# Rows of V at 144 bytes instead of 132, and a planner with other constants, in a multi-query attention kernel

## The chip, the core and the metric

The kernel runs on one core of a Trainium2 chip. The metric is the device time of one execution in microseconds (us). The core has five engines that run beside each other and meet at semaphores: TensorE (PE, matrix products), VectorE (DVE), ScalarE (ACT), GpSimd (POOL) and SyncE (SP, which here only issues transfers). Matrix products are written to PSUM, everything else that is kept on the chip lies in SBUF, both with 128 partitions.

## The reference

Multi-query attention: 8 batches, 1024 positions, 16 query heads of 64 columns, and one K and one V per batch that all heads share. All inputs and the output are float32.

```python
batch, seq_len, embed_dim = (8, 1024, 1024)
num_heads = 16
head_dim = embed_dim // num_heads
...
scores = np.matmul(q, k.transpose(0, 1, 3, 2)) / np.sqrt(head_dim)
weights = np.exp(scores - np.max(scores, axis=-1, keepdims=True))
weights = weights / np.sum(weights, axis=-1, keepdims=True)
attn_out = np.matmul(weights, v)
```

## The kernel before

**Units.** Heads are worked in pairs. A unit is one pair, one chunk of 512 queries and one key tile of 128 keys; there are 8 batches x 8 pairs x 2 chunks x 8 key tiles = 1024 of them. `scores` (L256) makes the scores of a unit with two matmuls (one per head, 64 rows of the array each, L263) into a PSUM tile of 128 keys x 1024 queries; there are three such tiles. No maximum is subtracted; sums out of range are detected at the end and sent to a general path that this input does not take.

**Two ways to the exponential.** A unit goes to ScalarE or to VectorE. ScalarE takes one instruction (`scalar_exp`, L276) and leaves one fp16 weight tile, "wt". VectorE builds the exponential from the bits of the scaled score: `ve_bits` (L283) reads the PSUM tile and writes the integer form, `ve_mantissa` (L294) and `ve_power` (L304) cut it apart, `ve_square` (L315) squares the mantissa, and the product of mantissa square and value, the cube, is made in two parts, the first columns by GpSimd (`ve_cube`, L319) and the rest by VectorE (`ve_rest`, L327). What comes out are three weight tiles in one buffer, "we", which enter the value product with the factors 1, C0 and C3.

**Values.** V of a batch lies in SBUF as `vps`, a tile of [128 keys, 3 terms, 8 key tiles, row], where the three terms are V, C0 x V and C3 x V (`prep_v`, L251), and each row holds 64 columns of V and a column of the term's factor, which makes the sum of the weights beside the product. `value` (L387, matmul at L396) multiplies 128 x 128 weights by 65 columns of such a row. An output group (128 queries of one head) is the sum of 8 products for the eight key tiles, in the order of the key tiles, and of two more for each key tile that VectorE made: first the terms C0 of all these, then the terms C3. Seven groups share a PSUM bank, and there are two such banks. `inverse` (L345) takes the reciprocal of the sums of a bank and `finish` (L354) multiplies the seven groups by it, both on VectorE; SP stores the result.

**The order.** All instructions are issued in an order that `plan` (L467) works out when the kernel is built, with a model of durations in its constants: T_MM for a value product, T_ACT, VE_COST and so on. TensorE's stream alternates between scores of one to three units and a burst of value products. The constants that set the order, as far as the change touches them:

- N_W3 buffers for VectorE's weight tiles, RATE the greatest share of units that VectorE gets, VE_SLACK the backlog up to which VectorE is given a further one.
- NEXT: how long VectorE may stand idle for a pass that is not ready yet rather than take another one. HOLD: `ve_bits` is not preferred over the unfinished passes of an earlier unit until the time to that unit's square is above HOLD.
- MINC the fewest columns of a cube that GpSimd is given, REST the remainder at or under which VectorE takes the rest itself.
- WAIT: when a score tile may be issued if one only is free, against the time at which ScalarE runs dry. SAFE: how long after its modelled readiness a weight tile may be used by a value product.

`load_v` is issued by POOL at unit 30 of the batch before, `prep_v` comes due at unit 72 (SIDE).

Of the kernel before, what the change touches and what calls it, by code (L numbers as in the profile page):

```python
# [11 lines left out]
FP16 = mybir.dt.float16  # L12
# [10 lines left out]
C3 = 0.163818359375  # L23
CS = 2.1471603163479376
N_WT = 22
N_W3 = 7
N_M = 2
N_M2 = 3
T_PAIR = 214.0
T_IN = 96.0  # L30
T_OUT = 106.0
T_MM = 30.8
T_SCORE = 480.0
T_ACT = 917.0
ACT_DONE = 1110.0
# [19 lines left out]
    "finish": 542.0,  # L55
}
ORDER = {"bits": 0, "inverse": 1, "finish": 2}
NEXT = {"bits": 0.0, "inverse": 0.0, "finish": 120.0}
MINC = 96
REST = 640  # L60
LATE = 500.0
VSLOT = 1
DEFER = 12
HOLD = 700.0
VE_SLACK = 2100.0
V_END = 12
RATE = 0.225
NEAR = 2000.0
WAIT = 50.0
T_BITS = 1255.0  # L70
SAFE = 0.0


@with_exitstack
def attention_main(ctx, tc, q, k, v, out, flag):
# [13 lines left out]
    P = 128  # L89
    NKT = S // P  # L90
# [13 lines left out]
    consts = ctx.enter_context(tc.tile_pool(name="consts", bufs=1))  # L104
# [12 lines left out]
    ident16 = consts.tile([P, P], FP16, name="ident16")  # L117
    ones = consts.tile([P, 1], FP32, name="ones")
    rec_all = consts.tile([P, NG], FP32, name="rec_all")
    vps = [consts.tile([P, 3, NKT, 66], FP16, name=f"vp{i}") for i in range(2)]  # L120
    ok_all = consts.tile([P, B + GRP], FP32, name="ok_all")
    qf = consts.tile([P, NKT, P], FP32, name="qf")

# [343 lines left out]
    def plan():  # L467
        ops = []

        def emit(t, what, *args):  # L470
            ops.append((t, len(ops), what, args))
# [10 lines left out]
        wt_used = [0.0] * N_WT  # L482
        w3_used = [0.0] * N_W3
        m_used = [0.0] * N_M
# [26 lines left out]
        def late_free(i):  # L511

            if free[i] < float("inf"):
                return free[i]
            return max(t_ve, min(x[1] for x in todo)) + T_BITS

        def backlog():

            t = sum(VE_COST[k] for k, _ in chain) + VE_COST["rest"] * len(left)
            return t + sum(VE_COST[k] for _, k, _, _ in evict)  # L520

        def share(s):
# [5 lines left out]
            if v is not None:  # L528
                gs = max(t_gp, t_behind + GP_START, squared[v] + GP_START)
                n = min(int((s - gs - GP_FIX) / GP_COL) // 32 * 32, left[v])  # L530
                if n >= MINC:
                    lo = 2 * QCH - left[v]
# [12 lines left out]
        def vector_step(limit):  # L545
# [4 lines left out]
            for x in [(r, "bits", v, 0) for v, r in todo] + evict:  # L550
                r, what = x[:2]
                s = max(t_ve, r, min(w3_used) if what == "bits" else 0.0)
                key = (max(s, t_ve + NEXT[what]), ORDER[what], x[2])
                if best is None or key < best[0]:
                    best = (key, s, x)
            urgent = best is not None and (
                best[1] <= t_ve + NEXT[best[2][1]]
                and (best[2][1] == "bits" or behind is not None or best[2][0] < t_ve - LATE or not chain)
            )
            if urgent and best[2][1] == "bits" and not any(left.values()):  # L560
                t = 0.0
                for what, v in chain:
                    t += VE_COST[what]
                    if what == "square":
                        urgent = t > HOLD
                        break
            if not urgent and (
                chain or left and (flush or left[next(iter(left))] <= REST or u - next(iter(left)) > DEFER)
            ):
                what, v = chain[0] if chain else ("rest", next(iter(left)))  # L570
                old = next(iter(left), None)
                if old is not None and (
                    left[old] <= REST
                    or what == "square"
# [74 lines left out]
        def issue(t, first):  # L649
# [6 lines left out]
                and not todo  # L656
                and max(t_ve, s) + backlog() < s + T_SCORE + VE_SLACK
                and kinds.get(u - 1) != "V"
                and made_v < (u - NKT + 1) * RATE
                and min(w3_used) < s  # L660
# [35 lines left out]
        while h < H or u < STEPS:  # L696
# [7 lines left out]
            if n_free == 1:  # L704
                other = sorted(late_free(i) for i in range(3))[1]
                go = max(other, t_pe) + T_IN + T_SCORE > t_act + WAIT and t_pe + NEAR >= t_act - T_IN - T_SCORE
            if u < STEPS and go:
# [15 lines left out]
            if terms is not None:  # L723
# [3 lines left out]
                if r < float("inf"):  # L727
                    r += SAFE
                if n == 0 and gg % GB == 0:
                    r = max(r, bank_free[gg // GB % 2])  # L730
                if r <= t_pe:
                    s = t_pe + (T_OUT if mode == "s" else 0)
                    mode = "v"
                    emit(s, "value", gg, n)
                    t_pe = s + T_MM
                    n += 1
# [185 lines left out]
@with_exitstack  # L922
def kernel(ctx, tc, q, k, v, out):
    nc = tc.nc
    fp = ctx.enter_context(tc.tile_pool(name="flagp", bufs=1))
    flag = fp.tile([1, 1], I32, name="flag")
    attention_main(tc, q, k, v, out, flag)
    bad = nc.values_load(flag, min_val=0, max_val=1)
    with tc.If(bad != 0):
        attention_general(tc, q, k, v, out)  # L930
# [30 lines left out]
```

## Time and profile before

| what | us |
|---|---|
| median of 3 runs | 769.5 (769.27 to 770.57) |
| the profiled execution | 769.24 |
| its span, first to last instruction | 767.5 |
| PE busy | 753.1 |
| ACT busy | 748.6 |
| DVE busy | 733.0 |
| POOL busy | 360.0 |

In a row of a group, the names are output<-inputs, then the shapes, the count after the x, and behind the bar the busy time in us, the mean duration in ns and the idle time ahead of it with what ended that. A row of a timeline or of the chain of waits begins with its start and its length in us. PE's durations overlap, since matmuls are pipelined: the distance of two starts says what one costs, not its duration. The same holds for the passes of VectorE and ScalarE, whose ends overlap with the next start by some 80 to 120 ns. The granted TensorE clock was 0.998 of full speed.

### The profile page before, as it was taken

The numbers are of one execution on the slowest core, as the hardware profiler recorded it, in microseconds if no ns is written. First come the engines' busy times: TensorE is split into PE (matmuls) and PEld (weight loads), VectorE is DVE, ScalarE is ACT, GpSimd is POOL, SyncE is SP. The second block draws the span as 40 slices with busy tenths as digits, with TensorE's granted clock in tenths as the row PEclk, the third lists the DMA queues.
The fourth block names the chain that finished last, engine by engine and source line by source line (L and its number), as shares of the span: only waits on it lengthen the run. The fifth ranks groups of instructions, "written<-read, shape, count | busy, mean of one in ns | idle before, by whom it ended". The sixth has DMA issues, their size and how long they took to land.

```text
span 767.5 us, 31677 instructions
## 1 busy us (share of the span) xinstructions
PE 753.1 (98%) x13842; PEld 486.4 (63%) x13842; DVE 733.0 (96%) x1467; ACT 748.6 (98%) x804; POOL 360.0 (47%) x314
## 2 busy tenths in 40 slices
PE   6999999999999999999999999999999999999996
PEld 3556666666666666666666666666666666666665
DVE  3999999999999999999999999999999999999994
ACT  7999999999999999999999999999999999999994
POOL 4554444545445535444555443545444444444440
PEclk9999999999999999999999999999999999999999
DMA  9976427654356634795447552487544676212122
GB/s 182 153 110 109 91 66 119 111 112 98 78 98 111 114 71 95 95 133 92 83 86 119 113 112 70 92 112 114 105 77 93 101 120 100 58 44 57 30 57 73
DMA packets 168926, 73.91 MB, mean 96 GB/s; under 512 B 94032, under 2 KB 161616, under 8 KB 168784
## 3 DMA queue, kind: packets, MB, share of 16 engines
q1 hardware_dynamic: 149152, 53.76, 35.5%
q0 software_dynamic: 18576, 17.57, 17.9%
q8 instruction: 109, 1.79, 1.0%
q10 hardware_dynamic: 1056, 0.52, 0.3%
q14 instruction: 33, 0.27, 0.1%
HBM read 37.75 MB, written 33.55 MB: 93 GB/s over the span
## 4 chain that ended last, share of the span: by engine, by line
PE 95%; ACT 2%; DVE 1%; DMA 1%; issue 0%
PE ot L396 57%; PE sc L263 38%; ACT wt L276 2%; DMA qf<-in_q_dram 1%; DVE we L283 0%; PE otl L420 0%; DVE osb L354 0%; PE qps L216 0%; DVE rec_all L345 0%; ACT q_first L799 0%; DVE mm L315 0%; ACT qt L229 0%; DVE we L304 0%; DVE m L294 0%; PE cnt L837 0%
## 5 line engine op out<-in xcount | busy, mean ns | idle before, releaser
L276 ACT ACTIVATE wt<-sc 128x1024 f16<-128x1024 f32 x801 | 746.1, 1040 | 4.5 <-PE sc L263 3.6
L319 POOL TENSOR_TENSOR we<-we,mm 128x864 f16<-128x864 f16 (+5 forms) x229 | 315.4, 1377 | 386.3 <-DVE mm L315 148.2
L396 PE MATMUL ot<-vp,wt 128*128 128x65 f16 x6344 | 441.3, 194 | 0.0
L396 PE MATMUL ot<-vp,we 128*128 128x65 f16 x5352 | 431.3, 194 | 0.0
L396 PEld LDWEIGHTS <-wt 128*128 128x128 f16 x6344 | 323.4, 98 | 129.2 <-issue 129.2
L396 PEld LDWEIGHTS <-we 128*128 128x128 f16 x5352 | 313.0, 97 | 92.0 <-issue 89.7
L263 PE MATMUL sc<-qt,k2t 64*128 64x512 f16 x2048 | 353.0, 386 | 3.5 <-ACT wt L276 2.8
L283 DVE TENSOR_SCALAR we<-sc 128x1024 int16<-128x1024 f32 x223 | 272.0, 1220 | 6.0 <-PE sc L263 4.3
L315 DVE TENSOR_TENSOR mm<-m 128x1024 f16<-128x1024 f16 x223 | 152.4, 683 | 0.1
L263 PEld LDWEIGHTS <-k2t 64*128 64x128 f16 x2048 | 77.8, 93 | 46.8 <-issue 7.0
L354 DVE TENSOR_TENSOR osb<-ot,rec_all 128x448 f32<-128x448 f32 x146 | 90.8, 622 | 4.9
L294 DVE TENSOR_SCALAR m<-we 128x1024 int16<-128x1024 int16 x223 | 95.1, 427 | 0.3
L304 DVE TENSOR_SCALAR we<-we 128x1024 int16<-128x1024 int16 x223 | 93.4, 419 | 0.0
L327 DVE TENSOR_TENSOR we<-we,mm 128x160 f16<-128x160 f16 (+5 forms) x219 | 78.2, 357 | 0.1
L166 POOL DMA_DIRECT2D q<-in_q_dram x64 | 38.6, 604 | 2.1 <-DMA q_first<-in_q_dram 1.7
L345 DVE RECIPROCAL rec_all<-ot 128x7 f32<-128x7 f32 x146 | 29.0, 198 | 6.4 <-PE ot L396 5.5
L149 POOL DMA_DIRECT2D vp<-in_v_dram x8 | 7.2, 900 | 0.0
L200 PE MATMUL kps<-ident,k 128*64 128x128 f16 x16 | 1.3, 314 | 4.5 <-DVE k L191 4.5
L251 DVE TENSOR_SCALAR vp<-vp 128x512 f16<-128x512 f16 x16 | 3.9, 286 | 1.5 <-DMA vp<-in_v_dram 1.5
L229 DVE COPY qt<-qps 128x512 f16<-128x512 f16 (+1 forms) x2 | 1.1, 555 | 4.0 <-PE qps L216 4.0
L234 DVE TENSOR_SCALAR k16d<-knat 128x1024 f16<-128x1024 f32 x7 | 4.8, 684 | 0.0
L200 PEld LDWEIGHTS <-k 128*64 128x64 f16 x16 | 0.8, 158 | 4.7 <-DVE k L191 4.7
(30 smaller groups left out, 23.5 us busy)
## 6 DMA issues: line engine op xcount, KB each, us to landing
out_dram<-osb SPq DMA_DIRECT2D x109, 256.0 KB, 2.7
q<-in_q_dram POOLq DMA_DIRECT2D x56, 256.0 KB, 4.6
out_dram<-osb SPq DMA_DIRECT2D x38, 128.0 KB, 2.6
knat<-in_k_dram SPq DMA_DIRECT2D x7, 256.0 KB, 3.3
q<-in_q_dram POOLq DMA_DIRECT2D x8, 192.0 KB, 7.5
vp<-in_v_dram POOLq DMA_DIRECT2D x8, 128.0 KB, 6.6
qt<-q SPq DMA_TRANSPOSE x64, 5.2
qf<-in_q_dram ACTq DMA_DIRECT2D x2, 256.0 KB, 4.4
```

The lines of the kernel that those rows point to most:

```text
L166: nc.gpsimd.dma_start(out=q16[(b, c)], in_=q[b, c * P : (c + 1) * P, h0:, :].rearrange("p h d -> p (h d)"),)
L263: nc.tensor.matmul(sc[u][:, hh, :], k2t[r : r + 64, j * P : (j + 1) * P], qt[b][r : r + 64, p % HP, c * QCH : (c + 1) * QCH], start=True, ...
L276: nc.scalar.activation(out=w, in_=sc.pop(u), func=EXP, scale=escale, bias=math.log(CS))
L283: nc.vector.tensor_scalar(out=w3[:, 1].bitcast(I16), in0=sc.pop(u), scalar1=15.0 * 1024, scalar2=0.0, op0=ALU.add, op1=ALU.max,)
L294: return nc.vector.tensor_scalar(out=ve[u]["m"].bitcast(I16), in0=ve[u]["w3"][:, 1].bitcast(I16), scalar1=0x3FF, scalar2=0x3C00, op0=ALU.b ...
L304: return nc.vector.tensor_scalar(out=ve[u]["w3"][:, 0].bitcast(I16), in0=ve[u]["w3"][:, 1].bitcast(I16), scalar1=0x7C00, scalar2=None, op0 ...
L315: return nc.vector.tensor_tensor(out=ve[u]["m2"], in0=m, in1=m, op=ALU.mult)
L319: x = nc.gpsimd.tensor_tensor(out=wu[:, lo:hi], in0=we[:, lo:hi], in1=mm[:, lo:hi], op=ALU.mult)
L327: return nc.vector.tensor_tensor(out=wu[:, lo:], in0=we[:, lo:], in1=mm[:, lo:], op=ALU.mult)
L345: nc.vector.reciprocal(out=rec_all[:, g0 : g0 + n], in_=o[:, 0:n, D])
L354: nc.vector.tensor_tensor(out=ob[:, i0 : i0 + n, :], in0=o[:, 0:n, 0:D], in1=rec.unsqueeze(2).broadcast_to([P, n, D]), op=ALU.mult,)
L396: nc.tensor.matmul(ots[g0][:, gg - g0, 0 : D + 1], w[:, hh, qb * P : (qb + 1) * P], kv[h // (HP * NCH)]["vp"][:, ci, u % NKT, 0 : D + 1], ...
```

## The change

The rows of `vps` become 72 columns of fp16 long, 144 bytes, where they were 66 columns, 132 bytes; the columns that are written and read stay the same 65. The tile starts at a multiple of 64 bytes in both kernels. The constants of the planner change with it, and so does the order of nearly all instructions behind the first units.

```diff
-N_W3 = 7
+N_W3 = 8
...
-T_MM = 30.8
+T_MM = 29.6
...
-NEXT = {"bits": 0.0, "inverse": 0.0, "finish": 120.0}
-MINC = 96
-REST = 640
+NEXT = {"bits": 0.0, "inverse": 0.0, "finish": 0.0}
+MINC = 128
+REST = 768
...
-HOLD = 700.0
-VE_SLACK = 2100.0
+HOLD = 1400.0
+VE_SLACK = 2500.0
...
-RATE = 0.225
+RATE = 0.235
...
-WAIT = 50.0
+WAIT = -100.0
...
-SAFE = 0.0
+SAFE = 300.0
...
-    vps = [consts.tile([P, 3, NKT, 66], FP16, name=f"vp{i}") for i in range(2)]
+    vps = [consts.tile([P, 3, NKT, 72], FP16, name=f"vp{i}") for i in range(2)]
```

What the order of the built programs holds, counted:

| | before | after |
|---|---|---|
| units of ScalarE / VectorE | 801 / 223 | 800 / 224 |
| value products (L396) | 11,696 | 11,712 |
| bursts of them | 733 | 744 |
| score runs of 1 / 2 / 3 units | 453 / 276 / 2 | 475 / 264 / 4 |
| GpSimd cubes (L319): instructions, columns | 229, 144,320 | 279, 121,888 |
| VectorE rests (L327): instructions, columns | 219, 84,032 | 222, 107,488 |
| `finish` directly behind `inverse` | 145 | 7 |
| bits pass directly behind a square | 117 | 147 |

## The prediction

> **What bounds the kernel now.** I read the page first (shares, chain, groups), then the windows of the steady part, the chain of waits piece by piece, and last the timeline of single engines.
>
> ```profile
> span 767.5 us, 31677 instructions
> PE 753.1 (98%) x13842; PEld 486.4 (63%) x13842; DVE 733.0 (96%) x1467; ACT 748.6 (98%) x804; POOL 360.0 (47%) x314
> PE 95%; ACT 2%; DVE 1%; DMA 1%; issue 0%
> L276 ACT ACTIVATE wt<-sc 128x1024 f16<-128x1024 f32 x801 | 746.1, 1040 | 4.5 <-PE sc L263 3.6
> L396 PE MATMUL ot<-vp,wt 128*128 128x65 f16 x6344 | 441.3, 194 | 0.0
> L396 PE MATMUL ot<-vp,we 128*128 128x65 f16 x5352 | 431.3, 194 | 0.0
> L263 PE MATMUL sc<-qt,k2t 64*128 64x512 f16 x2048 | 353.0, 386 | 3.5 <-ACT wt L276 2.8
> ```
> ```profile
> 100.00:700.00 600.00, 600.00 (x11133) 388.68 (x11128) 591.21 (x1181) 597.09 (x641) 287.80 (x240) 1.00 0.55 96
> ```
>
> (The window's columns are length, then busy time of PE, weight loads, DVE, ACT, POOL, then clock and DMA.) Three engines are 98% busy or more, but the chain that ended last is PE for 95%, and PE's scores waited 3.5 us in all. So TensorE sets the end; ACT and DVE are just behind it. A matmul's 194 ns is its pipelined length, not what it costs; the cost is the distance between starts, which the chain of waits shows, since its pieces run from start to start:
>
> ```profile
> 470.65 0.54 PE sc L263 x4
> 471.19 1.32 PE ot L396 x39
> 472.52 0.54 PE sc L263 x4
> 473.05 0.39 PE ot L396 x9
> 473.45 0.32 PE sc L263 x2
> 473.77 0.63 PE ot L396 x17
> ```
>
> From x9 (0.385, the mean of the 0.38 and 0.39 that such pieces show) to x39 (1.32) is 0.935 us for 30 value products: **31.2 ns each**, and 1.32 - 39 x 0.0312 = 0.10 us for each burst, whatever its length. A unit's two score matmuls alone cost 0.32 us, two units together 0.54.
>
> **What the padding does.** A row of vp is the moving operand of one value product. In both kernels vp starts at a multiple of 64 bytes. With 132-byte rows, key tile j starts at phase 0, 4, 8, 12, 0, 4, 8, 12 of a 16-byte grid for j = 0 to 7 (each of the three term blocks repeats this); with 144 bytes every row starts at phase 0. The trace before already holds sequences of equal phase, because a group of products ends with the extra terms of the DVE tiles (names "we"). In the first rows DVE made tiles 0 and 4, so each "we x5" is five starts that follow a row of phase 0; in the second it made tiles 1 and 5, so "we x4" is four starts after rows of phase 4, while the rows between ("wt x1" up to the next "we x4") climb through all eight.
>
> ```profile
> 408.68 0.31 PE L396 MATMUL ot<-vp,we 128*128 128x65 f16 x5
> 408.83 0.26 PE L396 MATMUL ot<-vp,wt 128*128 128x65 f16 x3
> ...
> 409.05 0.31 PE L396 MATMUL ot<-vp,we 128*128 128x65 f16 x5
> 409.20 0.26 PE L396 MATMUL ot<-vp,wt 128*128 128x65 f16 x3
> ...
> 409.43 0.31 PE L396 MATMUL ot<-vp,we 128*128 128x65 f16 x5
> 409.58 0.26 PE L396 MATMUL ot<-vp,wt 128*128 128x65 f16 x3
> ```
> ```profile
> 735.14 0.28 PE L396 MATMUL ot<-vp,we 128*128 128x65 f16 x4
> 735.26 0.19 PE L396 MATMUL ot<-vp,wt 128*128 128x65 f16 x1
> ...
> 735.51 0.28 PE L396 MATMUL ot<-vp,we 128*128 128x65 f16 x4
> 735.63 0.19 PE L396 MATMUL ot<-vp,wt 128*128 128x65 f16 x1
> ...
> 735.89 0.28 PE L396 MATMUL ot<-vp,we 128*128 128x65 f16 x4
> 736.00 0.19 PE L396 MATMUL ot<-vp,wt 128*128 128x65 f16 x1
> ```
>
> Phase 0: 0.15 three times, 0.45 us for 15 starts, 30.0 ns. Phase 4: 0.12, 0.12, 0.11, that is 0.35 for 12, 29.2 ns. Climbing: 735.26 to 735.51 and 735.63 to 735.89, 0.51 for 16, 31.9 ns; and 408.83 to 409.05 with 409.20 to 409.43, 0.45 for 14, 32.1 ns. So the same engine, in the same microsecond, is some 2.4 ns faster where the phase does not climb. After the change I take 0.80 us / 27 = **29.6 ns** for every value product, with 29.2 and 30.0 as bounds.
>
> By the Trainium skill, page "TensorE: Matmul & The Clock Gate", section "Back-to-back issue gap", a stream of weight load and matmul pairs is paced by both, at some 81 ns for 128 columns. Then a V row's place would not matter; the trace's 31.2 ns does not bear that out.
>
> **TensorE's sum.** The order of the changed program (counted, no time in it) has 11,712 value products where there were 11,696, in 744 bursts where there were 733, and score runs of 475 single units, 264 pairs and 4 triples where there were 453, 276 and 2 (and one of four). Value products: 11,696 x 31.2 = 364.9 us become 11,712 x 29.6 = 346.7, -18.2. Bursts: 11 x 0.10 = +1.1. Scores: +22 x 0.32 - 12 x 0.54 + 2 x 0.76 - 0.98 = +1.1 (a triple as 0.54 + 0.22, the four as 0.98). Together **-16.0 us**. The profiled execution took 769.24 (its span 767.5 and 1.74 around it; the median of the runs is 769.5). TensorE alone would so end at **753.2**; with 29.2 ns at 748.5, with 30.0 ns at 757.9.
>
> **ScalarE's sum.** It makes 800 tiles where it made 801, because DVE gets 224 for 223.
>
> ```profile
> 7.34 7.45 ACT L276 ACTIVATE wt<-sc 128x1024 f16<-128x1024 f32 x8 [0.70 <-PE sc L263]
> 339.73 16.62 ACT L276 ACTIVATE wt<-sc 128x1024 f16<-128x1024 f32 x18
> 719.86 37.42 ACT L276 ACTIVATE wt<-sc 128x1024 f16<-128x1024 f32 x40
> ```
>
> Fed without a gap its pitch is (16.62 - 1.03) / 17 = 0.917 us (the first row gives the same); over the steady window it is 600 / 641 = 0.936, so it now waits 19 ns a tile for TensorE. It starts at 7.34, and from its end at 757.28 to the end of the span are 10.2 us. Fully fed: 7.34 + 799 x 0.917 + 1.03 + 10.2 + 1.74 = **753.0**. TensorE's whole gain can be used, with nothing to spare.
>
> **VectorE's sum.** This is where the refitted planner matters most. NEXT["finish"] 120 -> 0 lets it put another pass between the reciprocal and the multiply that needs its result: in the order of before a finish follows its reciprocal directly 145 times, in the changed one 7 times.
>
> ```profile
> 472.50 0.20 DVE L345 RECIPROCAL rec_all<-ot 128x7 f32<-128x7 f32 x1
> 472.74 0.62 DVE L354 TENSOR_TENSOR osb<-ot,rec_all 128x448 f32<-128x448 f32 x1
> 473.28 1.22 DVE L283 TENSOR_SCALAR we<-sc 128x1024 int16<-128x1024 f32 x1
> 474.41 0.24 DVE L327 TENSOR_TENSOR we<-we,mm 128x160 f16<-128x160 f16 x1
> 474.58 0.41 DVE L294 TENSOR_SCALAR m<-we 128x1024 int16<-128x1024 int16 x1
> ...
> 475.91 1.22 DVE L283 TENSOR_SCALAR we<-sc 128x1024 int16<-128x1024 f32 x1
> ```
> ```profile
> 221.42 0.20 DVE L345 RECIPROCAL rec_all<-ot 128x7 f32<-128x7 f32 x1
> 221.53 0.38 DVE L304 TENSOR_SCALAR we<-we 128x1024 int16<-128x1024 int16 x1
> ```
>
> Reciprocal to finish takes 0.24, reciprocal to an independent pass 0.11: 138 x 0.12 (starts are rounded to 0.01) = **-16.6 us**. Against it, MINC 128 and REST 768 move part of the cubes from GpSimd back to DVE: 107,488 columns of L327 in 222 instructions, where there were 84,032 in 219.
>
> ```profile
> L327 DVE TENSOR_TENSOR we<-we,mm 128x576 f16<-128x576 f16 x86 | 39.0, 453 | 0.0
> L327 DVE TENSOR_TENSOR we<-we,mm 128x160 f16<-128x160 f16 x99 | 24.3, 245 | 0.0
> ```
>
> (453 - 245) / 416 = 0.50 ns a column, so 23,456 columns are +11.7, and 3 x 0.16 of fixed cost +0.5. The one tile more (RATE and VE_SLACK come to no more than that) is a bits pass of 1.13 (473.28 to 474.41) and its three passes of 1.33 (474.58 to 475.91): +2.5. Sum +14.7, net **-1.9 us**. DVE's load so stays while the span is to shrink by 2%. It idles 8.8 of the 600 us in the window, about 10 over the run; if all of that went and 1.9 more, the end could come 11.9 earlier, at **757.3**. That is a bound on the safe side: a wait shorter than the overlap of two passes shows as busy, and DVE's last tiles end before ACT's, so some of the tail is slack. GpSimd gives up work (busy 47% now) and is no bound.
>
> **What costs nothing.** The V load writes the same 128 KB into wider rows; it is issued at unit 30 of a batch and needed at unit 72, 42 units x 0.75 us = 31 us ahead (767.5 / 1024 a unit), against this landing time (last column, us); without that cover the prepare pass would stand some 7 us per batch.
>
> ```profile
> vp<-in_v_dram POOLq DMA_DIRECT2D x8, 128.0 KB, 6.6
> ```
>
> The eighth w3 buffer costs memory alone. SAFE 300 and WAIT -100 only reorder products already counted; the cover is the queue of other ready products, and were it empty each of the 744 bursts could start up to 0.3 us late.
>
> **Sum.** 753.2, 753.0 and at most 757.3 for three engines, the largest decides, and three that all have nothing to spare wait for each other a little. I take **756.5 us**, nearest to the largest; own range 752 to 761.
>
> **Rivals.**
> 1. The gain sticks halfway: ACT's pitch falls only to 0.927, the middle of 0.917 and 0.936, as DVE and ACT wait in turn for score slots. 7.34 + 799 x 0.927 + 1.03 + 10.2 + 1.74 = 761.0. For it: 98.5% DVE, no reserve. Against: PE's waits for both are only 3.5 us now. Chance 0.18.
> 2. The padding does nothing, since the pitch has another cause: TensorE's sum is only the additions, 1.1 + 1.1 + 16 x 0.031 = +2.7, so 771.9. For it: the total 31.2 is near what any mix gives. Against: the two fences of phases. Chance 0.04. The Trainium skill, "SBUF — State Buffer", "Specifications (TRN2)", has 16-byte lines with a penalty for each new one; 130 bytes touch nine lines from phase 0, 4, 8 or 12 alike, so that count would give this rival's result, and the trace's 32 against 29.6 ns speaks against the count alone.
> 3. Slower, by the score slots: HOLD 1400 lets DVE finish a square (0.60 us) before it reads the next scores; bits follow a square 147 times for 117. A slot held longer starves ACT and PE. It decides once the mean delay passes 16.0 / 224 = 71 ns a DVE tile; at 30 more squares of 0.60, 18 us, it ends at 753.2 + 18 = 771. Against: PE's scores waited 3.5 us in all before, 2.8 of it for ACT, so at most 0.7 for DVE. Chance 0.05.
> 4. DVE gains nothing, since waits for TensorE fill the freed holes: its steady part stays and the time is about 769. Chance 0.06.
>
> **How the numbers follow.** The forecast's own case has 0.67. The range 751 to 763 takes in it but for its edges and most of rival 1; out of it stay rivals 2 to 4 (0.15) and a little. A measurement of this kernel tells 0.2% (1.5 us) from no change. Faster: 0.67 + 0.18 + 0.01 of rival 4 = 0.86; same: the rest of rival 4, 0.05; slower: rivals 2 and 3, 0.09.
>
> **What would show it.** In the profile after: a piece of some 39 to 41 products in the chain with (length - 0.10) / count near 29.6 ns; ACT's count in 100 to 700 us near 652 (600 / 0.92); reciprocals whose follower starts 0.11 later; PE no longer 95% of the chain but sharing it with ACT and DVE. A pitch over 31 ns, or score matmuls that wait more than 10 us for ACT or DVE, would make the prediction wrong.

## The result, and the profile after

The changed kernel takes 763.3 us (762.9 to 763.9, 4 runs), the kernel before 769.38 beside it: ratio 0.9919, 95% interval 0.9902 to 0.9937. It is faster, by 6.1 us or 0.8%; 12.9 were forecast, and the range ended at 763. The profiled execution took 762.94, of which the span is 761.1.

Lines of the page of the changed kernel: busy shares, the chain by engine, and the groups that answer to those of before.

```profile
span 761.1 us, 31746 instructions
PE 746.3 (98%) x13858; PEld 480.7 (63%) x13858; DVE 728.8 (96%) x1474; ACT 747.5 (98%) x803; POOL 327.2 (43%) x364
ACT 54%; PE 42%; issue 3%; DMA 1%; DVE 1%
L276 ACT ACTIVATE wt<-sc 128x1024 f16<-128x1024 f32 x800 | 745.0, 1046 | 1.1 <-PE sc L263 0.9
L263 PE MATMUL sc<-qt,k2t 64*128 64x512 f16 x2048 | 354.3, 385 | 4.4 <-ACT wt L276 2.9
```

The window from 100 to 700 us (length, busy time of PE, weight loads, DVE, ACT, POOL, clock, DMA):

```profile
100.00:700.00 600.00, 598.53 (x11187) 385.81 (x11184) 590.00 (x1190) 599.85 (x644) 262.93 (x285) 1.00 0.52 96
```

Two readings compete here. The chain has moved from PE (95%) to ACT (54%), as if ScalarE had become the bound. But PE's scores waited only 4.4 us in all, hardly more than the 3.5 of before, and ScalarE makes a tile every 600 / 644 = 0.932 us, far from the 0.917 that it needs when it is fed. An engine that is a bound would run at its own pace. The chain of waits, same stretch as before:

```profile
470.12 0.54 PE sc L263 x4
470.66 1.35 PE ot L396 x41
472.01 0.54 PE sc L263 x4
472.55 0.41 PE ot L396 x10
472.96 0.32 PE sc L263 x2
473.28 0.62 PE ot L396 x17
```

From x10 (0.41) to x41 (1.35) is 0.94 us for 31 products: **30.3 ns**, where 31.2 stood before and 29.6 were forecast. Scores cost 0.32 and 0.54 as before. What a burst looks like inside shows in the distances from start to start (ns), from the third product on in the bursts at 471.19 (before) and 470.66 (after):

```
before  29 29 34 32 33 29 33 33 32 29 30 29 32 29 34 32 33 29 32 33 33 29 30 29 29 29 36 33
after   29 29 29 29 35 29 30 29 29 35 29 29 29 30 35 29 29 29 29 35 29 30 29 29 35 29 29 29
```

Before, three rows in four of a climb mostly cost 32 to 34. With the key tiles of the whole trace told apart by the order of the terms, the next start comes 29.3 ns after a row at phase 0 and 33.4, 32.6 and 32.4 ns after rows at 4, 8 and 12, 31.9 in the mean of a climb. After, all rows are at phase 0, most cost 29, and about every fifth costs 35. Behind the fourth product of a burst (all bursts but the last) there are 8,677 distances; nearly all of them are 5,852 of 29, 1,193 of 30 and 1,626 of 35, and the mean is 30.27. Before, the same mean was 31.27, since 60% of those products stand in a climb and the rest cost 30.3.

VectorE's timeline, same stretch: the reciprocal (L345) now has another pass behind it, and that one starts 0.12 us later (473.73 to 473.85), where the finish started after 0.24.

```profile
473.73 0.19 DVE L345 RECIPROCAL rec_all<-ot 128x7 f32<-128x7 f32 x1
473.85 0.37 DVE L327 TENSOR_TENSOR we<-we,mm 128x512 f16<-128x512 f16 x1
474.14 0.62 DVE L354 TENSOR_TENSOR osb<-ot,rec_all 128x448 f32<-128x448 f32 x1
```

### The profile page after: what moved, and what is told of

Its sections match the earlier page's. It is cut to its first block, busy times and chain, and to the rows that moved or that the text cites. A ratio compares the mean times of both kernels' runs of the same rounds, so it can differ in the third digit from the quotient of the medians.

```text
span 761.1 us, 31746 instructions
## 1 busy us (share of the span) xinstructions
PE 746.3 (98%) x13858; PEld 480.7 (63%) x13858; DVE 728.8 (96%) x1474; ACT 747.5 (98%) x803; POOL 327.2 (43%) x364
## 4 chain that ended last, share of the span: by engine, by line
ACT 54%; PE 42%; issue 3%; DMA 1%; DVE 1%
ACT wt L276 54%; PE ot L396 24%; PE sc L263 17%; DMA knat<-in_k_dram 0%; PE otl L420 0%; DMA out_dram<-osb 0%; DVE osb L354 0%; PE kps L200 0%; PE qps L216 0%; DVE k L191 0%; DVE rec_all L345 0%; DVE k2t L212 0%; PE cnt L837 0%; DVE okm L835 0%; DVE ok_all L443 0%
## 5 line engine op out<-in xcount | busy, mean ns | idle before, releaser
L276 ACT ACTIVATE wt<-sc 128x1024 f16<-128x1024 f32 x800 | 745.0, 1046 | 1.1 <-PE sc L263 0.9
L319 POOL TENSOR_TENSOR we<-we,mm 128x448 f16<-128x448 f16 (+4 forms) x279 | 281.9, 1010 | 409.2 <-DVE mm L315 214.4
L396 PE MATMUL ot<-vp,wt 128*128 128x65 f16 x6336 | 432.2, 194 | 0.0
L396 PE MATMUL ot<-vp,we 128*128 128x65 f16 x5376 | 432.2, 194 | 0.0
L396 PEld LDWEIGHTS <-wt 128*128 128x128 f16 x6336 | 317.4, 97 | 115.0 <-issue 115.0
L396 PEld LDWEIGHTS <-we 128*128 128x128 f16 x5376 | 316.1, 97 | 104.5 <-issue 103.4
L263 PEld LDWEIGHTS <-k2t 64*128 64x128 f16 x2048 | 80.1, 93 | 48.5 <-issue 7.8
L294 DVE TENSOR_SCALAR m<-we 128x1024 int16<-128x1024 int16 x224 | 92.5, 413 | 0.2
L354 DVE TENSOR_TENSOR osb<-ot,rec_all 128x448 f32<-128x448 f32 x146 | 89.2, 611 | 0.2
L327 DVE TENSOR_TENSOR we<-we,mm 128x576 f16<-128x576 f16 (+7 forms) x222 | 87.4, 394 | 0.0
L345 DVE RECIPROCAL rec_all<-ot 128x7 f32<-128x7 f32 x146 | 28.7, 197 | 7.4 <-PE ot L396 6.8
```

Of the source, the lines that this page charges most:

```text
L263: nc.tensor.matmul(sc[u][:, hh, :], k2t[r : r + 64, j * P : (j + 1) * P], qt[b][r : r + 64, p % HP, c * QCH : (c + 1) * QCH], start=True, ...
L276: nc.scalar.activation(out=w, in_=sc.pop(u), func=EXP, scale=escale, bias=math.log(CS))
L294: return nc.vector.tensor_scalar(out=ve[u]["m"].bitcast(I16), in0=ve[u]["w3"][:, 1].bitcast(I16), scalar1=0x3FF, scalar2=0x3C00, op0=ALU.b ...
L319: x = nc.gpsimd.tensor_tensor(out=wu[:, lo:hi], in0=we[:, lo:hi], in1=mm[:, lo:hi], op=ALU.mult)
L327: return nc.vector.tensor_tensor(out=wu[:, lo:], in0=we[:, lo:], in1=mm[:, lo:], op=ALU.mult)
L345: nc.vector.reciprocal(out=rec_all[:, g0 : g0 + n], in_=o[:, 0:n, D])
```

## The experiments

**The two halves apart.** The padding alone on the kernel before, and the new constants alone with 132-byte rows.

```diff
 pad_only, against the kernel before
-    vps = [consts.tile([P, 3, NKT, 66], FP16, name=f"vp{i}") for i in range(2)]
+    vps = [consts.tile([P, 3, NKT, 72], FP16, name=f"vp{i}") for i in range(2)]
 plan_only, against the changed kernel
-    vps = [consts.tile([P, 3, NKT, 72], FP16, name=f"vp{i}") for i in range(2)]
+    vps = [consts.tile([P, 3, NKT, 66], FP16, name=f"vp{i}") for i in range(2)]
```

> The kernel before with 144-byte rows alone, its order and constants untouched. Theory A (TensorE is still the bound, and a stream of products at phase 0 pays 29 ns with some 35 ns every fifth one, 30.3 on average): the pitch inside bursts is 30.3 ns as in the changed kernel, 10,963 pitches x 0.9 ns = 9.7 us less, so about 760 us. Theory B (the rest of the gain was lost at the handing over of scores, ScalarE being 54% of the chain): the old order cannot use the shorter products and it stays above 765.

> The changed kernel's order with 132-byte rows. Theory A: the pitch goes back to 31.3 ns, the 11 bursts more cost 1 to 5 us, so 770 to 774. Theory B: the relief of VectorE (reciprocal and finish apart) shows by itself, and it comes out between 762 and 768.

Measured: pad_only 760.19 (759.62 to 761.15; ratio 0.9887, 0.9870 to 0.9903), plan_only 772.01 (771.60 to 773.47; ratio 1.0046, 1.0032 to 1.0060), beside 768.87 for the kernel before. The padding is worth 8.7 us, the constants cost 3.1, and both numbers come out the same whichever half they are added to: 763.3 - 760.2 = 3.1 and 772.0 - 763.3 = 8.7. (The changed kernel ran at another time than these two; by the ratios the padding is worth 8.7 and 9.8, and the constants cost 3.5 and 2.5.) TensorE's distances from start to start say where: inside bursts they add up to 342.1 us in pad_only and 341.7 in the changed kernel, while those from score to score, into a burst and out of it are 398.9 and 402.1. So Theory A: TensorE's sum sets the end in all four kernels, and the new order only has more of it. Page and chain of pad_only:

```profile
span 758.6 us, 31677 instructions
PE 86%; DVE 9%; ACT 3%; issue 1%; DMA 0%; DVEq 0%
L276 ACT ACTIVATE wt<-sc 128x1024 f16<-128x1024 f32 x801 | 738.3, 1067 | 4.0 <-PE sc L263 3.3
```
```profile
604.41 1.29 PE ot L396 x39
...
606.24 0.41 PE ot L396 x10
```

(1.29 - 0.41) / 29 = 30.3 ns: the changed kernel's pitch under the old order. The chain names PE again, for the same pitch and nearly the same time. In plan_only it names ACT for 63%, at a time 9 us longer than the changed kernel's:

```profile
ACT 63%; PE 32%; issue 3%; DMA 1%; DVE 0%
```

Where two engines run in lock step, as here, the chain's choice between them is no verdict on which is slower.

**A planner told the measured pitch.**

```diff
 tmm304, against the changed kernel
-T_MM = 29.6
+T_MM = 30.4
```

> The changed kernel with the planner told 30.4 ns for a value product, which is what the burst shows. Same products (11,712), 751 bursts for 744. Theory A: TensorE's sum changes by 7 bursts x 0.2 us, so 763 to 765, no gain from the better fitted plan. Theory B: the plan fits the chip better, waits shrink and it comes out at 758 or less.

Measured: 762.51 (762.05 to 763.32; ratio 0.9919, 0.9903 to 0.9936), just below the 763 to 765 of Theory A; its runs overlap with the changed kernel's 762.9 to 763.9, and the ratio is the same. Its chain names PE for 91%, where the changed kernel's names ACT for 54% at nearly the same time. The fit of this one constant was not what was missing.

**VectorE's part undone.**

```diff
 next120, against the changed kernel
-NEXT = {"bits": 0.0, "inverse": 0.0, "finish": 0.0}
+NEXT = {"bits": 0.0, "inverse": 0.0, "finish": 120.0}
```

> The changed kernel with NEXT finish at 120 again, so that finish follows its reciprocal directly as before (the planner then makes 11,680 products in 745 bursts). The prediction counted on VectorE's 16.6 us. Theory A (TensorE sets the end in the changed kernel too): 32 products fewer are worth 1 us, and VectorE's loss lies beside it, so 761.5 to 764.5. Rival (VectorE is at its limit and carries the end): 770 or more.

Measured: 764.55 (763.83 to 765.19; ratio 0.9938, 0.9921 to 0.9955), against 0.9919 (0.9902 to 0.9937) for the changed kernel: 1.2 us by the medians, 1.5 by the ratios, with 32 products fewer (1 us), and the intervals overlap. Its row of the finish has the idle time back that the changed kernel's lost (5.1 us and 0.2):

```profile
L354 DVE TENSOR_TENSOR osb<-ot,rec_all 128x448 f32<-128x448 f32 x146 | 90.6, 621 | 5.1 <-DVE rec_all L345 0.4
```
```profile
L354 DVE TENSOR_TENSOR osb<-ot,rec_all 128x448 f32<-128x448 f32 x146 | 89.2, 611 | 0.2
```

(The first row is next120's, the second the changed kernel's.) VectorE's 16.6 us were there: from the reciprocals to the passes behind them are 33.9 us in next120 and 17.9 in the changed kernel. They were worth some 2 us. The rival is out.

**What sets the pitch.** Four kernels with other lengths of the stream. All use the changed kernel's order, so TensorE's instructions are the same but for the length.

```diff
 narrow33 and narrow57 (with 8 for 32), against the changed kernel
+        x0 = 0 if n == 0 else 32
         nc.tensor.matmul(
-            ots[g0][:, gg - g0, 0 : D + 1],
+            ots[g0][:, gg - g0, x0 : D + 1],
             w[:, hh, qb * P : (qb + 1) * P],
-            kv[h // (HP * NCH)]["vp"][:, ci, u % NKT, 0 : D + 1],
+            kv[h // (HP * NCH)]["vp"][:, ci, u % NKT, x0 : D + 1],
 cols64: both slices x0 : 72 with x0 = 8; wide72: both 0 : 72; in both also
-            nc.gpsimd.memset(t[:, i, :, D : D + 1], ci)
+            nc.gpsimd.memset(t[:, i, :, D:], ci)
```

> All value products but the first of each group stream only 33 columns (32 to 64, the sums among them); so columns 0 to 31 of the output hold the first key tile alone. If the length of the stream sets the pitch (Theory A with a free weight load), it falls by some 13 ns and TensorE is no bound any more: the time then shows what ScalarE and VectorE need, 753 by the prediction's sums. If pairs of weight load and matmul have a floor of their own at 30.4 ns, the pitch stays at 30.3 and the time at 763. Theory B: the time stays at 760 or above though the pitch falls.

> The changed kernel with products of 57 columns (8 to 64) after a first one of 65 in each group; columns 0 to 7 of the output hold the first key tile alone. A stream of 57 columns is 8 / 2.4 = 3.3 ns shorter by the difference of the runs with 65 and 33 columns at most. If the extra 6 ns belong to rows that end 2 bytes into a new 16-byte piece, they are here too (56 columns are whole pieces, the 57th begins one): a mean of 26 to 27 ns with a share of pitches 5 to 7 ns above the rest. If they belong to 65 columns alone, the pitch is even.

> The changed kernel with products of 64 columns (8 to 71 of a row, the spare ones filled with the term's factor) after a first one of 72 in each group; so columns 0 to 7 of the output hold the first key tile alone. What the extra 6 ns at every fifth product hang on: if on the 65th column (a last piece of the row with 2 bytes in it), they go, and the pitch inside bursts is even, 28.8 to 29.2 ns; the time falls to 753 to 757, as it does for any product that is 1.3 ns shorter. If they come with every stream whatever its length, every fifth pitch stays at 35 and the mean at 29.9 or above.

> The changed kernel with products of 72 columns, the whole 144-byte row; the output is unchanged. The stream is 7 columns, some 2.9 ns, longer than 65. If a product costs its columns and the 6 ns come from the ragged end, the pitch is even at 32.1 ns, no 35s, and TensorE's sum grows by 1.8 ns x 10,968 = 20 us, to 780 to 785. If the 6 ns come every fifth product whatever the length, the mean is 33.3 and the time about 795.

Pieces of the chain of narrow57 (a piece of 41 and one of 10: 0.83 us for 31 products, 26.8 ns), then of cols64 (29.4 ns) and wide72 (32.6 ns):

```profile
210.14 1.21 PE ot L397 x41
...
212.64 0.38 PE ot L397 x10
```
```profile
106.24 0.40 PE ot L397 x10
...
111.80 1.31 PE ot L397 x41
```
```profile
100.46 1.44 PE ot L396 x41
...
102.44 0.43 PE ot L396 x10
```

| columns | pitch from the pieces, ns | distances behind the fourth product | time, us |
|---|---|---|---|
| 33 | - | 25 and 26, some 29; mean 25.6 | 752.3 |
| 57 | 26.8 | 26 to 28, some 29; mean 27.0 | 752.7 |
| 64 | 29.4 | 29 to 32; mean 29.5 | 753.1 |
| 65 (changed kernel) | 30.3 | 29, 30 and 35; mean 30.3 | 763.3 |
| 72 | 32.6 | 32 and 33; mean 32.6 | 787.7 |

(One run each but for the changed kernel.) The first product of each group is longer in the kernels with 33, 57 and 64 columns, and it stands in these figures: the same 771 places hold the 31s and 32s of cols64 and nearly all the 29s and 30s of the two narrow ones. Without them 33 columns go at 25.2 ns, 57 at 26.8 and 64 at 29.2, and the last is even, 29 or 30; 72 columns go at 32.5 but for 34 gaps of 60 ns. The 35s are gone at 57, 64 and 72 columns: of the lengths tried they belong to 65 alone. Not to every stream, and not to rows that end 2 bytes into a new 16-byte piece either, since 57 columns from a multiple of 16 bytes do that too. So the floor of 30.4 for a pair of weight load and product is out, for 33 columns go at 25.2. But narrow33 fell by 5 ns where some 13 were expected: from 57 to 33 columns the pitch loses 1.5 ns only, so the length no longer sets it there. From 57 to 72 a column costs (32.6 - 26.8) / 15 = 0.39 ns, which puts 65 at 29.9; from 64 to 72 it is (32.5 - 29.2) / 8 = 0.41, which puts it at 29.6. The 35s are thus mostly the way in which 65 columns come to their mean, and only the last 0.4 to 0.7 ns are a loss. wide72 missed its expected 780 to 785, as its pitch is 0.5 ns above the 32.1 expected.

The Trainium skill, "TensorE: Matmul & The Clock Gate", "Back-to-back issue gap", has columns / 2.4 + 2.5 ns for an isolated matmul, with a floor of some 25 ns, and says that this is too little for a stream of weight loads and short matmuls. Estimates by that formula are 26.3, 29.2, 29.6 and 32.5 ns for 57, 64, 65 and 72 columns. The runs, with a weight load for every product, have 26.8, 29.2, 30.3 and 32.5, and 25.2 for 33. So the isolated rule fits this stream to 0.5 ns at the other lengths, and is least right, by 0.7 ns, at the one length that this kernel uses.

The three short ones also show what lies behind TensorE: they all end at 752.3 to 753.1, however short the product. ScalarE is then fed; the page and window of narrow57:

```profile
ACT 82%; PE 12%; issue 5%; DMA 1%; DVE 0%; ACTq 0%
L276 ACT ACTIVATE wt<-sc 128x1024 f16<-128x1024 f32 x800 | 733.9, 1287 | 2.1 <-PE sc L263 2.1
```
```profile
100.00:700.00 600.00, 592.61 (x11377) 385.44 (x11376) 596.98 (x1208) 599.74 (x656) 267.40 (x289) 1.00 0.52 97
```

600 / 656 = 0.915 us a tile. And the mean length of an activation is 1,287 ns for the same work that takes 1,046 in the changed kernel. The recorded lengths grow with the overlap: they are 1,300 in the mean where an activation starts more than 200 ns before the end of the one ahead (759 of narrow57's 800), and 1,023 for the changed kernel's 52 that start less than 20 ns before that end, or later. So it seems that one that finds its scores early starts early and stands behind the one ahead. The column is a sign of a backlog, which busy shares (both 98%) are not; it is no measure of one, for cols64 has 1,103 at nearly the same time.

**The phase itself.** V from another column of the 144-byte row, so that all rows are at equal phase, but not 0.

```diff
 phase8, against pad_only (phase4 with 2 for 4, phase12 with 6)
-            out=vps[b % 2][:, 0, :, 0:D], in_=v[b].rearrange("(c p) d -> p c d", p=P)
+            out=vps[b % 2][:, 0, :, 4 : D + 4], in_=v[b].rearrange("(c p) d -> p c d", p=P)
...
-                out=vp[:, i, :, 0:D], in0=vp[:, 0, :, 0:D], scalar1=ci, scalar2=None, op0=ALU.mult
+                out=vp[:, i, :, 4 : D + 4], in0=vp[:, 0, :, 4 : D + 4], scalar1=ci, scalar2=None, op0=ALU.mult
...
-            kv[h // (HP * NCH)]["vp"][:, ci, u % NKT, 0 : D + 1],
+            kv[h // (HP * NCH)]["vp"][:, ci, u % NKT, 4 : D + 5],
...
-                    vp[:, i, j, 0 : D + 1],
+                    vp[:, i, j, 4 : D + 5],
...
-                nc.gpsimd.memset(t[:, i, :, D : D + 1], ci)
+                nc.gpsimd.memset(t[:, i, :, D + 4 : D + 5], ci)
```

> The kernel before with 144-byte rows in which V starts at column 4, so every row starts at phase 8 of the 16-byte grid instead of phase 0. If what costs time is the climb from one phase to the next, equal phase is enough: pitch 30.3 ns in bursts and about 760, as with phase 0. If a row has to start at a multiple of 16 bytes, the pitch is 31.3 or more and the time 769 or more.

> The kernel before with 144-byte rows in which V starts at column 2, so every row is at phase 4. If the start phase sets the size of the slip at every fifth product, as 0 (35 to 36 ns, mean 30.35) and 8 (33 to 34, mean 29.9) suggest, a value of its own comes out: the sequences of phase 4 in the trace before had 29.2, so 29.2 to 29.9 and a time of 749 + ScalarE's limit of 754, that is 754 to 756.5. If phase does not matter and phase 8 was chance, 30.3 and 760.

> The same with V from column 6, phase 12. If the start phase sets the slip, the mean follows the sequences of equal phase 12 in the trace before, which had 30 to 31 ns: 760 or a little more. If any equal phase but 0 gives 29.9, 756.

| rows at phase | distances behind the third product | mean, ns | time, us |
|---|---|---|---|
| 0 (pad_only) | 29, 30, the slip 35 | 30.35 | 760.2 |
| 4 | 29, 30, the slip 32 or 33 | 30.04 | 758.0 |
| 8 | 29, 30, the slip 33 or 34 | 29.91 | 756.2 |
| 12 | 29, 30, the slip 34 or 35 | 30.16 | 759.2 |

Phase 8 in the chain, (1.28 - 0.38) / 30 = 30.0 ns:

```profile
114.27 1.28 PE ot L396 x39
116.09 0.38 PE ot L396 x9
```

A row need not start at a multiple of 16 bytes: equal phase is what the padding bought, and phase 0 has the longest slips and the highest mean of the four. In time, phase 12 is only 1.0 us from it, with one run. The means hold a few gaps of 54 to 57 ns, 26, 31 and 34 of them at phases 0, 4 and 12 and none at 8. Without these the four are 30.27, 29.95, 29.91 and 30.06 for phases 0, 4, 8 and 12, so phases 4 and 8 can hardly be told apart. phase4 missed the expected 754 to 756.5 and phase12 the 760; the slip shrinks at both, by less and by more than the short sequences in the trace before had led to expect. Phases 4, 8 and 12 have one run each; the next paragraph has phase 8 with four.

**Versions that use it.** Constants of before, 144-byte rows.

```diff
 rate220, against pad_only (phase8_rate220: the same against phase8)
-RATE = 0.225
+RATE = 0.220
 wait150, against pad_only
-WAIT = 50.0
+WAIT = 150.0
 rate220_w100, against pad_only
-RATE = 0.225
+RATE = 0.220
-WAIT = 50.0
+WAIT = 100.0
```

> 144-byte rows with the constants of before and RATE 0.220: two units fewer for VectorE, 11,664 products in 727 bursts. Theory A (TensorE sets the end, by counted rows): 32 products x 0.030 and 6 bursts x 0.1 fewer, scores 0.6 us less, so 2.2 us under the 760.2 of the rows alone, 758. ScalarE's own limit with 803 tiles is 755.7. Rival (VectorE or ScalarE sets the end there): 760 or more.

> 144-byte rows with the constants of before and WAIT 150: the same 11,696 products in 718 bursts for 733, more scores in pairs. Theory A: 15 bursts x 0.1 and 1.5 us of scores fewer, so 757.1. If the later scores leave ScalarE dry instead, 760 or more.

> 144-byte rows with the constants of before, RATE 0.220 and WAIT 100: 11,664 products in 704 bursts. Theory A: 1.0 us of products, 3.0 of bursts and 2.9 of scores fewer than with the rows alone puts TensorE at 753.3, below ScalarE's 755.7, so about 756 and no engine left with a reserve. If the handing over of scores costs more than the switches saved, 760 or more.

> 144-byte rows with V from column 4 (phase 8), the constants of before and RATE 0.220. If phase 8 is real, TensorE's sum is that of rate220 less 10,937 x 0.4 ns = 4.4 us, 753.3, and ScalarE's limit with 803 tiles is 755.7: so 755 to 756.5, under every kernel so far. If phase 8 was chance, 757.7 again.

Measured: rate220 757.67 (ratio 0.9856, 0.9839 to 0.9872), wait150 760.61 (0.9886, 0.9867 to 0.9904), rate220_w100 759.98 (0.9880, 0.9864 to 0.9897), phase8_rate220 **755.87** (754.67 to 756.50; 0.9818, 0.9802 to 0.9834), by its median the fastest of all that keep the whole computation. The first and the last came as counted. The two with a greater WAIT did not. Over 1,330 and 1,344 steps from one score matmul to the next TensorE spends 79.9 and 85.6 us, over pad_only's 1,315 steps 75.8. Most of that is no loss: a step to the next unit's scores costs 0.22 us, so the 15 and 29 bursts less bring 3.3 and 6.5 us of such steps themselves, and with these counted they still saved 2.1 and 4.1 us. But 0.8 and 3.3 us more are spent between scores, and 1.4 and 1.0 us more between the value products, and that took the saving back. The row of the scores shows some of it as waits for ScalarE, that is for a free PSUM tile. It stands here for rate220_w100, and for rate220 behind it:

```profile
L263 PE MATMUL sc<-qt,k2t 64*128 64x512 f16 x2048 | 349.8, 386 | 6.6 <-ACT wt L276 4.5
```
```profile
L263 PE MATMUL sc<-qt,k2t 64*128 64x512 f16 x2048 | 351.2, 385 | 4.1 <-ACT wt L276 2.9
```

## Why the prediction was off, step by step

- **What bounds the kernel: right, and longer than forecast.** TensorE set the end before, and still does after. The forecast let VectorE's 757.3 decide.
- **The padding: right in its direction and its cause, mis-sized in its price.** The step that failed is "After the change I take 0.80 us / 27 = 29.6 ns for every value product, with 29.2 and 30.0 as bounds". It measures 30.3, above the upper bound. The 27 starts came from sequences of four and five, and pooled two phases: the phase-0 rows alone had given 30.0, and the phase-4 rows 29.2. More such starts would not have helped. The kernel before has no run of equal phase that is longer than five rows, and all 1,927 distances in such runs (behind the fourth product of a burst) have a mean of 29.7. At phase 0 none of the 286 up to the fourth row is a 35, and 29 of the 78 to the fifth row are. So the slip was nearly out of sight. Products then are 11,712 x 30.3 = 354.9 us instead of 346.7, so 8.2 of the 18.2 us were not there; with it TensorE's sum would have been 753.2 + 8.2 = 761.4. The changed kernel's profiled execution took 762.9. Added up over the two profiles, the distances inside bursts went from 351.4 to 341.7 us, -9.7 where -18.2 was forecast.
- **Bursts and scores: right in kind, and a little short.** +2.2 us were counted for the new order. TensorE's distances from score to score, into a burst and out of it went from 398.2 to 402.1 us, +3.9, and the constants cost 3.1 by pad_only and plan_only.
- **ScalarE's limit of 753.0: right.** 752.3, 752.7 and 753.1 when the products are too short to matter. In the changed kernel it was simply not reached.
- **VectorE: the mechanism was right, the bound was none.** Reciprocal and next pass did move to 0.12 us apart. But "at most 757.3 for three engines, the largest decides" took an upper bound, in which busy time holds hidden waits, for what VectorE needs: narrow57 has the changed kernel's order for VectorE too and ends at 752.7, and next120 gives all the holes back and ends at 764.55. The 3.3 us that it put on top of TensorE's 753.2 went in the right direction for the wrong reason.
- **Rivals.** The first, ScalarE's pitch stuck between 0.917 and 0.936, happened by its number (0.932) but not by its reason: not waits in turn, but a longer product. The second fell with pad_only. For the third, PE's scores waited 4.4 us instead of 3.5, so it was not seen. The fourth is half true: VectorE's freed holes did bring next to nothing, though the time fell.

What stays open is why 65 columns slip at about every fifth product (at phase 4 every fourth) and why the slip's size goes with the start phase. That the slip hangs on the length (none at 64 and 72) and on the phase (35, 32 to 33, 33 to 34, 34 to 35) is shown; a cause in the chip is not.

## What to carry to other kernels

When an instruction that runs ten thousand times is priced, take the mean over long sequences of exactly the form it will have. Where the trace at hand has none, widen the bounds or run the change by itself: starts in fours and fives gave 29.6 ns for a product that costs 30.3, and 0.7 ns x 11,712 = 8.2 us is most of TensorE's miss of 10 (forecast -16.0, measured -9.7 + 3.9 = -5.8). Try the change in layout without the new constants as well: here the layout alone was 3.1 us faster than the two together, and the best version kept the old order. And where two engines run in lock step, read the bound from what a shorter instruction on one of them does to the time, not from the chain's shares.

## What the runs showed of the hardware

- The pitch of a stream of weight load and product of 65 columns depends on how the start phase of the moving row goes on from product to product: 31.9 ns in the mean when it climbs by 4 bytes each time (the kernel before), 29.9 to 30.35 when it stays (pad_only and the three phases).
- At equal phase 65 columns of fp16 run at 29 or 30 ns with a slip to 32 to 35 at about every fifth product; 64 columns run evenly at 29.2 and 72 at 32.5.
- A product of 33 columns costs 25.2 ns, hardly less than one of 57 (26.8) though 24 columns shorter.
